# A conditioned two-layer decoder on one core: features a step earlier, shorter norms, and other first loads

## Chip, core and metric

The kernel runs on one core of one Trainium2 chip. The metric is the device time of one execution in microseconds (us); the time given for a kernel is the median of its runs.

## What is computed

Two transformer layers of width 2048 over 256 tokens, float32, batch 1. Every layer is a mixer and a squared-ReLU MLP of hidden width 8192, each with a modulated norm ahead of it and a gate behind it:

```
for l in (0, 1):
    shift, scale, gate, shift2, scale2, gate2 = split(silu(c) @ ada_w[l] + ada_b[l])   # 12288 columns
    h = rms_norm(x, norm_mix_g[l]) * (1 + scale) + shift
    x = x + gate * mixer(l, h)          # 0: MoBA + sliding window (GQA, sinks); 1: FoX + NSA
    h = rms_norm(x, norm_mlp_g[l]) * (1 + scale2) + shift2
    x = x + gate2 * (relu(h @ up[l]) ** 2 @ down[l])
out = rms_norm(x, final_norm_g)
```

The even mixer projects h to 4608 columns: eight MoBA heads' q, k and v, and eight sliding-window q heads with two k and v heads; with 256 tokens MoBA is causal attention inside one block.

## The kernel before

**Data.** x is kept transposed in xT: 16 feature blocks of 128, each 128 x 256 tokens. The modulated, normed features are in xs, per block a float32r high part (256 columns) and the rest, the low part (256 columns). A matrix product is three matmuls per pair of blocks: high x high, low x high, high x low.

**Weights.** `load` (L312) brings weights in pieces of 128 x 1024 words (0.5 MB) into the pool wst, tag "w", of eight buffers. ACT copies each piece to its high part wh (L319), DVE subtracts for the low part wl (L321). The wl instruction frees the buffer. All weight loads are issued by SP, in order.

**Modulation (ada).** `queue` puts one generator per section pair or column range into the list fill; `ada` (L222) is the generator. Sections are 0 shift, 1 scale, 2 gate of the mixer, 3, 4, 5 the same of the MLP. Each step loads 0.5 MB of ada_w into a wst buffer and multiplies it with cond: on PE (row, L238) where tensor is True, else on DVE (acc, L242 and L245, 128 x 1024). After the last step `columns` (L256) puts blocks into the list late: four transposes on PE, a reduction (L265) and a few small DVE instructions that write mod. `tick` (L293) is called once per weight load: it takes one entry of late and pumps 2 x rate steps of ada. `need(left, keys)` (L301) pumps until the sections named are through, and empties late.

**First layer's projection.** `even` (L615) goes over five groups of feature blocks, K1_GROUPS = 2, 2, 4, 4, 4 blocks, named 0 to 4 here. A group has nine calls of `kproj` (L374), each of which loads 512 columns of W for the group's blocks, ticks, seeds its PSUM tiles with the sum so far, multiplies and copies the sum out. The features of group g need the shift and scale of its columns; groups 0 and 1 have them from PE steps, 2 to 4 from DVE steps:

```
for g, (k0, kn) in enumerate(K1_GROUPS):
    need(end - g, (0, 1))
    ia, iv = make_h(0, 0, 1, Rs, range(k0, k0 + kn))
    rate[0] = R_K1[g]
```

In group 4 the sixteen attention heads follow their projections (`swa`, `moba`). `up_streamed` (L671) does the same for the first half of the first MLP's up projection: four groups of four blocks, eight kprojs each.

**Norms.** `residual` adds to xT and squares it on ACT (L147); DVE adds the squares to sacc (L151). `sumsq` (L440) sums over partitions by matmuls with ones (L444, L445), per half j of the tokens first sacc, then the last square t. `rstd` (L433) takes the power on POOL (L437). `norm_scale` (L448) makes the diagonal dg on DVE (L453) and multiplies ones with it (L454), so that R holds each token's factor on all partitions; with keep, ACT copies R to Rs (L456). `make_h` (L459) makes per block t = xT * scale * R on DVE (L463), high on ACT (L464), low on DVE (L465). `lazy_h` (L470) leaves it to `proj` (L348) to make four blocks per group of weights. `down` (L499) is the output and down projection: four blocks of columns, four weight loads and ticks each.

**Order.** Each engine runs its instructions in the order chosen when the kernel is built, by the program's order and by when an instruction could start by then-known costs; `issue_after` adds an order between two instructions of one engine.

**Start.** SP issues constants, x in eight loads of 128 x 512 (L162) into the pool big, and the tables of C_TRI (L163); ACT issues c and the small rows (L164 to L168). After group 0's make_h ACT issues the tables cos, sin and masks (L205) and the sinks. `norm_scale` here needs ones, which are in C_TRI.

Of the kernel before, what the change touches and what calls it, by code (L numbers as in the profile page):

```python
# [12 lines left out]
F32 = mybir.dt.float32  # L13
# [27 lines left out]
R_K1 = (0.6, 0.75, 0.9, 0.9, 1.6)  # L41
# [41 lines left out]
def build(tc, consts, x, c, norm_mix_g, norm_mlp_g, ada_w, ada_b, mlp_up, mlp_down, even_w_in, even_sinks,  # L83
# [5 lines left out]
    with ctx:  # L89
# [68 lines left out]
        xtok = [[None] * 4 for _ in range(2)]  # L158
        for q in range(4):
# [19 lines left out]
        for q in range(4):  # L179
            for j in range(2):  # L180
                junk = wrk.tile([128, 1024], F32, tag="acc", name="junk")
                A.activation(junk[:, 0:512], xtok[j][q], AF.Square, accum_out=ssq[:, 4 * j + q:4 * j + q + 1])
            for h in range(2):
                ps = psm.tile([128, 2, S], F32, tag="mm", name="xps")
                k0 = 4 * q + 2 * h
                for kk in range(2):
                    for j in range(2):
                        T.transpose(ps[:, kk, 128 * j:128 * j + 128], xtok[j][q][:, 128 * (2 * h + kk):128 * (2 * h + kk) + 128], ident)
                V.tensor_copy(xT[:, k0:k0 + 2, :], ps)
        ss0 = s32()  # L190
        V.tensor_reduce(ss0[:, 0:2], ssq[:, 0:8].rearrange("p (j q) -> p j q", q=4), AX.X, ALU.add)
# [12 lines left out]
        def later_vectors():  # L204
            A.dma_start(cst[:, 0:C_TRI], consts[:, 0:C_TRI])  # L205
            srow = att.tile([1, 8], F32, tag="srow", name="srow")
            A.dma_start(srow, even_sinks)
            A.dma_start(fb, fox_forget_b.rearrange("o h -> h o"))
# [13 lines left out]
        def ada(l, secs, c0, cw, tensor):  # L222
            cols = cw * len(secs)
            kn = KS * 512 // cols
# [4 lines left out]
            for t in range(KT // kn):  # L229
                w = wst.tile([128, kn, cols], F32, tag="w", name="wa")  # L230
                for z, s in enumerate(secs):
                    SP.dma_start(w[:, :, cw * z:cw * z + cw], ada_w[l, 128 * kn * t:128 * kn * (t + 1), D * s + c0:D * s + c0 + cw].rearrange("(k p) n -> p k n", p=128))
                for i in range(kn):
                    k = kn * t + i
                    hold = after("V")
                    if tensor:
                        q = 32 * (k % 4)
# [710 lines left out]
```

## Time and profile before

| | |
|---|---|
| median of 3 runs | 2288.84 us (2287.96 to 2292.45) |
| profiled execution | 2290.15 us |
| its span, first to last instruction | 2288.4 us |
| mean granted clock of TensorE | 0.985 of full |
| busy: PE, PEld, DVE, ACT | 97%, 94%, 73%, 52% |
| DMA | 600.06 MB, mean 262 GB/s |

PE is TensorE's matmuls, PEld its weight loads, DVE VectorE, ACT ScalarE, POOL GpSimd, SP SyncE, which only issues. L399 is line 399 of the kernel. PEclk is the granted TensorE clock as a share of 2.4 GHz; it is granted at that or at 1.2 GHz. An entry "[4.54 <-ACT xs L464]" means that the engine stood idle for 4.54 us and that the instruction of line 464 on ACT, which writes xs, ended it. PE's busy time runs together where matmuls overlap, so the count behind x is the better measure of its work.

### The profile page before, as it was taken

The numbers are of one execution on the slowest core, as the hardware profiler recorded it, in microseconds if no ns is written. First come the engines' busy times: TensorE is split into PE (matmuls) and PEld (weight loads), VectorE is DVE, ScalarE is ACT, GpSimd is POOL, SyncE is SP. The second block draws the span as 40 slices with busy tenths as digits, with TensorE's granted clock in tenths as the row PEclk, the third lists the DMA queues.
The fourth block names the chain that finished last, engine by engine and source line by source line (L and its number), as shares of the span: only waits on it lengthen the run. The fifth ranks groups of instructions, "written<-read, shape, count | busy, mean of one in ns | idle before, by whom it ended". The sixth has DMA issues, their size and how long they took to land.

```text
span 2288.4 us, 45838 instructions
## 1 busy us (share of the span) xinstructions
PE 2216.7 (97%) x18602; PEld 2147.1 (94%) x18602; DVE 1662.1 (73%) x2341; ACT 1180.4 (52%) x1873; POOL 5.6 (0%) x25
## 2 busy tenths in 40 slices
PE   8899999899999999999999999999999999999998
PEld 4799889899999999999999989899999999999997
DVE  3887899988877788887777977887545555555555
ACT  3766974578844354354454555444444444443543
POOL 0000000000000000000000000000000000000000
PEclk9999999999999999999999999999999999999999
DMA  9999679999998988988858876985555656555652
GB/s 320 312 333 322 242 258 364 326 355 364 328 317 276 319 290 300 312 306 295 262 184 296 313 253 222 325 313 159 193 198 190 199 190 201 188 198 189 199 185 93
DMA packets 296246, 600.06 MB, mean 262 GB/s; under 512 B 24706, under 2 KB 41954, under 8 KB 296034
## 3 DMA queue, kind: packets, MB, share of 16 engines
q1 hardware_dynamic: 295488, 596.38, 76.5%
q8 instruction: 146, 2.39, 0.4%
q10 hardware_dynamic: 546, 0.75, 0.1%
q14 instruction: 66, 0.54, 0.1%
HBM read 594.95 MB, written 2.10 MB: 261 GB/s over the span
## 4 chain that ended last, share of the span: by engine, by line
PE 47%; issue 33%; DVE 8%; DMA 7%; ACT 4%; SPq 0%; DVEq 0%; POOLq 0%; POOL 0%; ACTq 0%
PE mm L333 30%; PE mm L399 12%; DMA wa<-in_ada_w_dram 5%; DVE wl L321 3%; DVE acc L245 2%; PE bank L399 1%; ACT wh L319 1%; DMA w<-in_odd_w_in_dram 1%; PE row L238 1%; DMA w<-in_even_w_in_dram 1%; PE cps L263 1%; ACT u L402 1%; ACT mm L383 0%; PE bank L605 0%; ACT hs L417 0%
## 5 line engine op out<-in xcount | busy, mean ns | idle before, releaser
L321 DVE TENSOR_TENSOR wl<-w,wh 128x1024 fp32r<-128x1024 f32 x736 | 881.6, 1221 | 421.3 <-ACT wh L319 417.2
L319 ACT ACTIVATE wh<-w 128x1024 fp32r<-128x1024 f32 x736 | 754.1, 1055 | 771.4 <-PE mm L333 666.6
L333 PE MATMUL mm<-hs,wh 128*128 128x256 f32 x5120 | 881.3, 277 | 0.4 <-DVE xT L481 0.4
L333 PEld LDWEIGHTS mm<-hs,wh 128*128 128x128 f32 x5120 | 772.6, 188 | 1.6 <-DVE xT L481 1.0
L333 PE MATMUL mm<-xs,wh 128*128 128x256 f32 (+1 forms) x4128 | 717.8, 279 | 3.1 <-ACT xs L464 3.0
L333 PE MATMUL mm<-hs,wl 128*128 128x256 f32 x2560 | 708.3, 277 | 4.1 <-DVE wl L321 4.1
L333 PEld LDWEIGHTS mm<-xs,wh 128*128 128x128 f32 (+1 forms) x4128 | 626.3, 188 | 6.4 <-ACT xs L464 4.5
L333 PE MATMUL mm<-xs,wl 128*128 128x256 f32 x2064 | 571.7, 278 | 0.4 <-DVE wl L321 0.3
L245 DVE SCALAR_TENSOR_TENSOR acc<-wa,cond,acc 128x1024 f32<-128x1024 f32 x330 | 423.1, 1282 | 98.1 <-DMA wa<-in_ada_w_dram 96.3
L333 PEld LDWEIGHTS mm<-hs,wl 128*128 128x128 f32 x2560 | 481.0, 188 | 5.1 <-DVE wl L321 4.9
L333 PEld LDWEIGHTS mm<-xs,wl 128*128 128x128 f32 x2064 | 387.6, 188 | 1.5 <-DVE wl L321 1.0
L399 PE MATMUL mm<-xs,wh 128*128 128x256 f32 x1792 | 315.2, 280 | 6.0 <-ACT wh L319 4.2
L399 PEld LDWEIGHTS mm<-xs,wh 128*128 128x128 f32 x1792 | 273.2, 190 | 16.4 <-ACT wh L319 5.4
L399 PE MATMUL mm<-xs,wl 128*128 128x256 f32 x896 | 249.1, 279 | 1.5 <-DVE wl L321 1.5
L399 PEld LDWEIGHTS mm<-xs,wl 128*128 128x128 f32 x896 | 169.2, 190 | 2.2 <-DVE wl L321 2.1
L402 ACT ACTIVATE u<-mm 128x512 f32<-128x512 f32 x144 | 84.1, 592 | 73.9 <-PE mm L399 73.0
L383 ACT ACTIVATE mm<-u 128x512 f32<-128x512 f32 x112 | 65.5, 597 | 1.2
L548 ACT ACTIVATE t<-mm 128x256 f32<-128x256 f32 x96 | 36.5, 380 | 31.5 <-PE mm L333 26.2
L147 ACT ACTIVATE t<-xT 128x256 f32<-128x256 f32 x60 | 24.6, 415 | 51.3 <-DVE xT L481 51.3
L577 ACT ACTIVATE p<-p,st 128x128 f32<-128x128 f32 (+1 forms) x96 | 40.1, 420 | 19.7 <-DVE st L591 10.0
L399 PE MATMUL mm<-wh,xs 128*128 128x256 f32 x256 | 49.4, 286 | 0.1
L343 PE MATMUL mm<-wh,xs 128*128 128x256 f32 (+1 forms) x128 | 43.7, 342 | 0.0
(213 smaller groups left out, 1408.4 us busy)
## 6 DMA issues: line engine op xcount, KB each, us to landing
wa<-in_ada_w_dram SPq DMA_DIRECT2D x256, 512.0 KB, 5.2
w<-in_mlp_up_dram SPq DMA_DIRECT2D x256, 512.0 KB, 4.4
w<-in_mlp_down_dram SPq DMA_DIRECT2D x256, 512.0 KB, 4.9
wa<-in_ada_w_dram SPq DMA_DIRECT2D x256, 256.0 KB, 5.1
w<-in_odd_w_in_dram SPq DMA_DIRECT2D x88, 512.0 KB, 4.7
w<-in_even_w_in_dram SPq DMA_DIRECT2D x72, 512.0 KB, 5.4
w<-in_even_w_out_dram SPq DMA_DIRECT2D x32, 512.0 KB, 5.7
w<-in_odd_w_out_dram SPq DMA_DIRECT2D x32, 512.0 KB, 5.5
```

The costliest lines, as they stand in the source:

```text
L147: A.activation(s, xT[:, kt, :], AF.Square)
L238: T.matmul(row[q:q + 32, :], cond[:, k:k + 1].to_broadcast([128, 32]), w[:, i, :], start=k < 4, stop=k >= KT - 4, tile_position=(0, q))
L245: V.scalar_tensor_tensor(acc, w[:, i, :], cond[:, k:k + 1], acc, op0=ALU.mult, op1=ALU.add)
L319: A.activation(wh, w, AF.Copy)
L321: V.tensor_tensor(wl, w, wh.bitcast(F32), op=ALU.subtract)
L333: T.matmul(P[0:m, 0:S], st[:, c0:c0 + m], mv, start=f and i == 0, stop=e and i == 2)
L343: T.matmul(Ps[j][:, 0:n], lo, wh[:, c0:c0 + n], start=False, stop=e)
L383: A.activation(P, flat[i], AF.Copy)
L399: T.matmul(Ps[i][:, 256 * h:256 * h + 256], st, mv, start=first and e == 0, stop=last and e == 2, skip_group_check=True)
L402: A.activation(flat[i], P, AF.Copy)
L548: A.activation(r, P[:, 0:S], AF.Relu)
L577: A.activation(p[:, o:o + n], p[:, o:o + n], AF.Exp, bias=m[:, i:i + 1], accum_out=den[:, i:i + 1])
```

## The change

The features of the next group are made ahead of the group's last kproj (groups of four blocks) or last two (groups of two) in `even`, and ahead of the last kproj in `up_streamed`; the rates of groups 0 and 1 rise. ada loads shift and scale in one load where a step has one feature block, and in groups 0 and 1, whose steps are now twice as large, each section into its own buffer; the order of the two sections is turned. The norm's factor comes from a matmul of the broadcast r with the identity, without dg; R is always copied to Rs; `sumsq` takes sacc for both halves first; the last load of the last column block of a `down` that ends in a norm has no tick. The first `proj` behind a `lazy_h` goes over the feature blocks outermost for its first group. x comes in four loads of 128 x 1024 into wst; C_TRI comes with the later tables, which SP issues at the end of group 1.

```
-R_K1 = (0.6, 0.75, 0.9, 0.9, 1.6)
+R_K1 = (0.65, 0.9, 0.9, 0.9, 1.6)
...
-                xtok[j][q] = big.tile([128, 512], F32, tag="b", name="xtok")
-                SP.dma_start(xtok[j][q], x[0, 128 * j:128 * j + 128, 512 * q:512 * q + 512])
-        SP.dma_start(cst[:, C_TRI:C_ID], consts[:, C_TRI:C_ID])
...
+        xtok = [[wst.tile([128, 1024], F32, tag="w", name="xtok") for _ in range(2)] for _ in range(2)]
+        for q in range(2):
+            for j in range(2):
+                SP.dma_start(xtok[q][j], x[0, 128 * j:128 * j + 128, 1024 * q:1024 * q + 1024])
...
         def later_vectors():
-            A.dma_start(cst[:, 0:C_TRI], consts[:, 0:C_TRI])
+            SP.dma_start(cst[:, 0:C_ID], consts[:, 0:C_ID])
...
         def ada(l, secs, c0, cw, tensor):
             cols = cw * len(secs)
-            kn = KS * 512 // cols
+            split = len(secs) == 2 and cw == 256
+            kn = KS * 512 // (cw if split else cols)
...
+                for z, s in enumerate(secs if split else secs[0:1]):
+                    w = wst.tile([128, kn, cw if split else cols], F32, tag="w", name="wa")
+                    if kn == 1:
+                        SP.dma_start(w[:, 0, :].rearrange("p (s n) -> p s n", n=cw), src[:, 0, secs[0]:secs[-1] + 1, c0:c0 + cw])
                     else:
+                        SP.dma_start(w, src[:, :, s, c0:c0 + cw])
...
+            fresh = len(hgen) == 4
...
+                if fresh and g == 0:
+                    for k in range(4):
+                        for mt in range(4):
+                            mm_T(Ps[0][1][mt], ws[k:k + 1], 128 * mt, 128, xs_rhs(k, 1), k == 0, False)
+                    continue
...
-            for j in range(2):
-                T.matmul(ps[:, j:j + 1], sacc[:, 128 * j:128 * j + 128], ones[:, 0:1], start=True, stop=False)
-                T.matmul(ps[:, j:j + 1], sq[:, 128 * j:128 * j + 128], ones[:, 0:1], start=False, stop=True)
+            for t in (sacc, sq):
+                for j in range(2):
+                    T.matmul(ps[:, j:j + 1], t[:, 128 * j:128 * j + 128], ones[:, 0:1], start=t is sacc and j == 0, stop=t is sq and j == 1,
+                             skip_group_check=True)
...
-            dg = t256()
             for j in range(2):
-                V.tensor_scalar(dg[:, 128 * j:128 * j + 128], ident, r[:, j:j + 1], None, op0=ALU.mult)
-            T.matmul(R[:, 0:S], ones, dg, start=True, stop=True)
-            if keep:
-                A.activation(Rs, R[:, 0:S], AF.Copy)
+                T.matmul(R[:, 128 * j:128 * j + 128], r[:, j:j + 1].to_broadcast([128, 128]), ident, start=True, stop=True)
+            A.activation(Rs, R[:, 0:S], AF.Copy)
...
+                with tc.issue_after(done[-2]) if len(done) > 1 else nullcontext():
+                    V.scalar_tensor_tensor(t, xT[:, k, :], mod[:, 6 * l + sc, k:k + 1], R, op0=ALU.mult, op1=ALU.mult)
...
-                hgen.append(lambda g=g: make_h(l, sh, sc, R, range(4 * g, 4 * g + 4)))
+                hgen.append(lambda g=g: make_h(l, sh, sc, Rs if g else R, range(4 * g, 4 * g + 4)))
...
-                    tick()
+                    if not (sums and blk == 3 and n == 3):
+                        tick()
...
+            def features(g):
+                need(end - g, (0, 0))
+                k0, kn = K1_GROUPS[g]
+                return make_h(0, 0, 1, Rs, range(k0, k0 + kn))
+
+            features(0)
             for g, (k0, kn) in enumerate(K1_GROUPS):
-                need(end - g, (0, 1))
-                ia, iv = make_h(0, 0, 1, Rs, range(k0, k0 + kn))
...
                     kproj(W, g, 512 * b, [(256 * i, "T", qa[b][i]) for i in range(2)], k0, kn)
+                    if b == 1 and g < end and kn == 2:
+                        features(g + 1)
                     kproj(W, g, 1024 + 512 * b, [(256 * i, "T", ka[b][i]) for i in range(2)], k0, kn)
...
+                    if b == 1 and g < end and kn == 4:
+                        features(g + 1)
                     kproj(W, g, 2048 + 512 * b, [(0, j, va[b][j]) for j in range(2)], k0, kn)
...
-                if g == 0:
-                    with tc.issue_after(ia.ins):
-                        srow = later_vectors()
+                if g == 1:
+                    srow = later_vectors()
+                if g == 2:
                     sinks(srow)
...
                 for b in range(4 * K2C):
+                    if g < 3 and b == 4 * K2C - 1:
+                        features(g + 1)
```

## Rows read from the trace of the kernel before

**Rows 1.** The page's first part: busy time, share of the span and instructions of each engine.
```profile
PE 2216.7 (97%) x18602; PEld 2147.1 (94%) x18602; DVE 1662.1 (73%) x2341; ACT 1180.4 (52%) x1873; POOL 5.6 (0%) x25
```

**Rows 2.** Table by stretch (A:B length, engines' busy us, PEclk, DMA share, GB/s).
```profile
core 0: us, PE busy (x) PEld busy (x) DVE busy (x) ACT busy (x) POOL busy (x), PEclk, DMA share, GB/s
28.00:222.00 194.00, 175.85 (x1377) 162.55 (x1378) 143.12 (x158) 126.89 (x189) 0.00 (x0) 0.95 0.91 323
107.00:164.00 57.00, 53.19 (x441) 52.96 (x442) 48.15 (x52) 39.39 (x59) 0.00 (x0) 0.95 0.95 340
164.00:222.00 58.00, 56.16 (x459) 53.80 (x459) 44.73 (x47) 37.46 (x55) 0.00 (x0) 0.95 0.85 299
180.00:200.00 20.00, 20.00 (x177) 20.00 (x176) 17.20 (x15) 14.93 (x22) 0.00 (x0) 1.00 1.04 383
222.00:260.00 38.00, 37.93 (x285) 30.15 (x285) 25.23 (x62) 28.97 (x65) 0.00 (x0) 1.00 0.80 278
260.00:318.00 58.00, 50.61 (x359) 45.81 (x358) 53.17 (x126) 51.93 (x120) 0.00 (x0) 0.97 0.64 222
318.00:412.00 94.00, 93.98 (x808) 92.64 (x806) 92.24 (x127) 43.73 (x69) 0.00 (x0) 1.00 0.99 353
484.00:534.00 50.00, 50.00 (x443) 50.00 (x442) 45.26 (x48) 39.66 (x59) 0.00 (x0) 1.00 0.99 356
```

**Rows 3.** PE's waits, whole span (who <- what ended it: us, times, longest).
```profile
PE bank L399 <- ACT xs L464: 10.8, 4, 4.5
PE aux L454 <- DVE t L453: 7.1, 4, 2.6
...
PE aux L444 <- DVE sacc L151: 4.2, 3, 3.1
PE mm L333 <- ACT xs L464: 3.0, 3, 1.1
```

**Rows 4.** Timeline at the boundary from group 1 to 2 (start us, us, engine, line).
```profile
106.14 1.27 DVE L463 SCALAR_TENSOR_TENSOR t<-xT,mod,sacc 128x256 f32<-128x256 f32 x3
...
107.22 0.58 PE L399 MATMUL bank<-xs,wh 128*128 128x256 f32 x1 [4.54 <-ACT xs L464]
```

**Rows 5.** Table by stretch, around that boundary and around the first norm.
```profile
104.00:112.00 8.00, 4.78 (x23) 4.79 (x24) 8.00 (x17) 4.28 (x8) 0.00 (x0) 0.57 0.71 217
415.00:426.00 11.00, 7.80 (x34) 6.74 (x35) 9.32 (x17) 2.20 (x5) 1.62 (x1) 0.53 0.77 275
```

**Rows 6.** The chain that ended last: a stretch of group 2, one of group 4.
```profile
115.18 44.03 PE mm L399 x384
...
245.22 1.84 PE row L238 x12
```

**Rows 7.** What SP's queue waited for before issuing, 0 to 222 us.
```profile
SPq L232 <- DVE wl L321: 32.7, 23, 3.7
...
SPq L232 <- DMA cst<-in_consts_dram: 5.6, 1, 5.6
SPq L232 <- DMA xtok<-in_x_dram: 3.9, 2, 2.8
```

**Rows 8.** The page's costliest groups: busy us, mean ns of one behind the bar.
```profile
L321 DVE TENSOR_TENSOR wl<-w,wh 128x1024 fp32r<-128x1024 f32 x736 | 881.6, 1221 | 421.3 <-ACT wh L319 417.2
...
L245 DVE SCALAR_TENSOR_TENSOR acc<-wa,cond,acc 128x1024 f32<-128x1024 f32 x330 | 423.1, 1282 | 98.1 <-DMA wa<-in_ada_w_dram 96.3
```

**Rows 9.** Timeline of SP's queue at the start.
```profile
9.16 11.01 SPq L232 DMA_DIRECT2D wa<-in_ada_w_dram  x16
```

**Rows 10.** Timeline at the first norm (behind the even layer's output projection).
```profile
415.59 0.57 PE L444 MATMUL aux<-cst,sacc 128*128 128x1 f32 x2
...
418.51 0.48 DVE L453 TENSOR_SCALAR t<-cst,s 128x128 f32<-128x128 f32 x2 [0.58 <-POOL s L437]
...
420.37 0.38 ACT L456 ACTIVATE sacc<-aux 128x256 f32<-128x256 f32 x1 [5.51 <-PE aux L454]
420.79 1.26 DVE L463 SCALAR_TENSOR_TENSOR t<-xT,mod,aux 128x256 f32<-128x256 f32 x3 [0.60 <-ACT sacc L456]
```

**Rows 11.** Timeline at the second norm (ahead of the odd layer's mixer).
```profile
1142.65 1.26 DVE L463 SCALAR_TENSOR_TENSOR t<-xT,mod,aux 128x256 f32<-128x256 f32 x3 [0.85 <-PE aux L454]
```

More of the change, by code (lines that the diff above doesn't have):

```diff
@@ L229, in ada @@
             for t in range(KT // kn):
[L230 to L237, printed above, removed]
-                        T.matmul(row[q:q + 32, :], cond[:, k:k + 1].to_broadcast([128, 32]), w[:, i, :], start=k < 4, stop=k >= KT - 4,
-                                 tile_position=(0, q))
-                    elif k == 0:
-                        with hold:
-                            V.tensor_scalar(acc, w[:, i, :], cond[:, 0:1], None, op0=ALU.mult)
-                    else:
-                        with hold:
-                            V.scalar_tensor_tensor(acc, w[:, i, :], cond[:, k:k + 1], acc, op0=ALU.mult, op1=ALU.add)
+                src = ada_w[l, 128 * kn * t:128 * kn * (t + 1), :].rearrange("(k p) (s n) -> p k s n", p=128, n=D)
@@ new lines, in ada @@
+                for z, s in enumerate(secs if split else secs[0:1]):
+                    w = wst.tile([128, kn, cw if split else cols], F32, tag="w", name="wa")
+                    if kn == 1:
+                        SP.dma_start(w[:, 0, :].rearrange("p (s n) -> p s n", n=cw), src[:, 0, secs[0]:secs[-1] + 1, c0:c0 + cw])
+                    else:
+                        SP.dma_start(w, src[:, :, s, c0:c0 + cw])
+                    for i in range(kn):
+                        k = kn * t + i
+                        hold = after("V")
+                        if tensor:
+                            q, n = 32 * (k % 4), cw if split else cols
+                            T.matmul(row[q:q + 32, n * z:n * z + n], cond[:, k:k + 1].to_broadcast([128, 32]), w[:, i, :],
+                                     start=k < 4 and z == 0, stop=k >= KT - 4 and (not split or z == 1), tile_position=(0, q), skip_group_check=True)
+                        elif k == 0:
+                            with hold:
+                                V.tensor_scalar(acc, w[:, i, :], cond[:, 0:1], None, op0=ALU.mult)
+                        else:
+                            with hold:
+                                V.scalar_tensor_tensor(acc, w[:, i, :], cond[:, k:k + 1], acc, op0=ALU.mult, op1=ALU.add)
@@ L672, in up_streamed, with features @@
             us = [u_tile() for _ in range(8 * K2C)]
+            def features(g):
+                need(3 - g, (l, 3))
+                return make_h(l, 3, 4, Rs if g else R, range(4 * g, 4 * g + 4))
+            ia, iv = features(0)
             for g in range(4):
-                need(3 - g, (l, 4))
-                ia, iv = make_h(l, 3, 4, Rs if g else R, range(4 * g, 4 * g + 4))
                 for b in range(4 * K2C):
+                    if g < 3 and b == 4 * K2C - 1:
+                        features(g + 1)
                     if g == 0 and b == 2 and GATE:
@@ L894, in build @@
         for g in range(4):
-            queue(0, (4, 3), False, 512 * g, 512)
+            queue(0, (3, 4), False, 512 * g, 512)
         for c0 in (0, 1024):
```

36 lines of the change are left out of this document (17 added, 19 removed).

## The prediction

> **What bounds the kernel now.** I read the page's engine shares first: PE is busy 97% of the span, so a change can win only where PE stands still or runs at a low clock [rows 1]. The table by stretch comes next: in the first layer's projection groups (28 to 222 us) PE has 175.9 of 194 us busy at 0.95 of its clock, while the DMA engines are 91% busy; in group 4 with its attention it has 37.9 of 38 and then 50.6 of 58; in the output projection after it (318 to 412) it has it all [rows 2]. What ends PE's waits in these groups is the feature step: four waits for the first xs, 10.8 us; the norms' waits on dg and on sacc add 7.1 and 4.2 us [rows 3]. The boundary at 107 us shows why: DVE starts the features at 106.14, only then, and PE starts at 107.22 after 4.54 us of nothing [rows 4]; the clock around it is 0.57 of full, so matmuls on both sides of the wait ran at the lower level of 1.2 GHz for part of the time [rows 5]. Without a wait, 384 matmuls take 44.03 us, 0.1147 each [rows 6].
>
> **Features a kproj or two earlier.** A group of four feature blocks is nine kprojs of 48 matmuls: 432 x 0.1147 = 49.5 us. The group that begins at 107 lasts 57 us and the next one 58 [rows 2, 4]; so about 16 us are over in these two, boundary waits, low clock and transposes together. With features(g+1) ahead of the last kproj, their cover is that kproj, 5.5 us of matmuls, against 8 x 0.42 = 3.4 us of DVE work for four blocks (three of their eight instructions take 1.27 us [rows 4]). What they need must be there: the ada steps of the next group. Before, nine ticks a group at the old rates pump 10.8 + 13.5 + 16.2 + 16.2 = 56.7 steps, and groups 1 to 4 need 8 + 16 + 16 + 16 = 56, so the last step comes at the boundary itself. After, the rates give 11.7 + 16.2 + 16.2 + 16.2 = 60.3, and 4 + 48 = 52 are needed (group 1's steps are twice as large), with the last one two or three ticks before features. The wait at the boundary should go; late next is the DMA.
>
> **What that costs the DMA.** (60.3 + 4) - 56.7 = 7.6 steps of 0.524 MB, 4.0 MB, are loaded ahead of group 4 that were not; the table adds 0.2 MB here (a step is 128 x 1024 words of 4 bytes). From 28 to 222 us the queues moved 323 GB/s x 194 us = 62.7 MB; now 66.9 MB. The tiles' release paces it: SP waits longest for DVE's wl [rows 7]. If the tiles in waiting at the end of group 3 are 2 MB fewer (they pile up at a boundary), 64.9 MB are to be moved. Rates seen: 323 over the groups, 340 in group 2, 353 in the output projection, which asks for as much, 383 in the best 20 us [rows 2]. I take 350, nearest to the stretch without boundaries: 185 us. DVE allows it: in group 2 it is busy 48.2 of 57 us, of which 18 wl at 1.22 and 16 acc at 1.28 are 42 [rows 2, 8], so some 51 us a group is its floor.
>
> **The first loads.** The first ada load goes out at 9.16 us, and its group's sixteen take 11.01 us to issue [rows 9]; SP waits 3.9 us for x landings and later 5.6 us for the tables, which go out on the other queue [rows 7]. Four x loads for eight, eight ada loads for sixteen, and the tables later on SP's own queue take most of it away. xtok now takes four of the eight w slots, so half of group 0's ada waits for the transposes: bounded by 0 and 6 us of gain, I take 4, by the 3.9 us row. One load in place of two at the other ada steps saves SP's issue time alone, which hides beside the waits above: 0.
>
> So group 4 begins at 28 - 4 + 185 = 209 to 211 us instead of 222: **-11 us**.
>
> **The last group.** About eight steps of section 2 on PE are already done, and eight more steps on DVE come in here. PE: three steps took 1.84 us on the chain [rows 6], so eight are 4.9 us off the front, where PE is bound (37.9 of 38 us). DVE: 8 x 1.28 = 10.3 us; it has 12.8 us idle in the first 38 us, but is busy 53.2 of 58 in the rest [rows 2]. Bounds: -5 (all covered, PE's part gained) and +10.3 (nothing covered). About half of the new steps fall in the first part: +5, less 3 of PE's 4.9: **+2 us**.
>
> **Norms.** In the first, without the last tick two accs of 1.28 us no longer stand among the sacc adds, against a wait of 3.1 us: 1.5 (0 to 2.5; wl of the next stage may take their place). Without dg, whose two instructions take 0.48: 0.5. Both sacc products ahead of both of t: 0.4 of the second pair's 0.57 [rows 10]. Of 11 us at 0.53 of the clock [rows 5] a shorter standstill may spare 1.0 (0 to 1.7). Sum **-3.4** (-0.9 to -5.1). In the second and third the same 0.5 and 0.4 go, but now R is copied there too: in the first norm it was ACT's copy, 0.38 us, that released DVE's first feature, in the second, without copy, PE itself [rows 10, 11]. So +0.4 each: **-0.5** each, **-1.0**. The Trainium skill (PSUM — Partial Sum Buffer, "PSUM bank collisions raise a hardware error") says that reads of one bank by two engines must be kept apart as well; by that the copy and the feature cannot be side by side, and the 0.4 stays; were they free to overlap, it would be -1.8 in place of -1.0. Blocks outermost in the first proj (fresh): 0, bounds 0 and -1.5: only three waits there in all, 3.0 us, are for xs [rows 3], and some of them stand at the very first block. Features ahead of the last kproj in up_streamed, the order inside make_h: 0, bounds -0.5 and +3 (three boundaries at one wl of 1.22), as PE is busy there in all of 50 us [rows 2]. Rest of the program: 0, give or take 2, from shifted ada steps.
>
> **Sum.** -11 + 2 - 3.4 - 1.0 = -13.4 us. The profiled execution took 2290.15 us, which gives 2276.7; it is 1.3 us over the median of the three runs, 2288.84. On that median: **2275 us**.
>
> **Rivals.** *The DMA gains little* (18%): 340 GB/s as in group 2 and no fewer tiles in waiting: 66.9 / 0.340 = 197 us, group 4 starts 1 us earlier, and -1 + 2 - 4.4 = -3.4: 2285. For it: DMA is 91% busy already. Against it: 353 and 383 elsewhere. *The extra load decides* (8%, slower): the rate stays at the groups' own 323, because slots, not boundaries, hold it: 66.9 / 0.323 = 207 us, group 4 starts at 231, +9 + 2 - 4.4 = +6.6: 2295. It ends slower once the rate is under about 334 (66.9 MB in 200 us). Against it: at the boundaries the queue is seen to drop, 299 in group 3 against 383 inside it [rows 2]. *The DMA runs as in its best stretch* (16%): 66.9 MB at 383 GB/s, 175 us; PE's own floor, 3 x 49.5 and some 15 us for the steps on PE, is not in the way: group 4 at 199, -23, and with 0 for the last group -27.4: 2261. The Trainium skill (DMA: Bandwidth & Descriptors, Specifications) gives about 358 GB/s as the memory's limit for a core; by it 66.9 MB take 187 us, group 4 starts at 211, and this rival is out. The trace does not agree: 383 over 20 us. *The change doesn't move the work* (4%): engines' orders are fixed when the kernel is built, and the features may end up where they were; then loads and norms gain 4 + 4.4, against 2 in the last group and 4.2 MB at 350 GB/s, 12 us, half of it in the boundaries' gaps: 2288.
>
> **How the numbers follow.** The forecast has 54%; its own range is 2265 to 2284 (rates of 343 to 360 give -9 to -18 for group 4's start; the bounds of the last group halved, norms). A measurement of this kernel can tell about 0.2%, 4.6 us, from no change. Faster by more: 54 + 16 + 10 of the first rival's 18 (its time lies on the border) = 80%. Within: 8 + 4 = 12%. Slower: 8%. The range 2263 to 2287 leaves out the slower rival, a good third of the 383 rival and the forecast's tails.
>
> **What would show it.** Right: no wait of PE's for xs over 2 us between groups; stretch rows of the groups over 340 GB/s; first matmul of the groups 4 us earlier, group 4 near 210, the output projection's end some 9 us earlier; PE's standstill at the first norm halved; DVE waiting for ACT's copy in all norms. Wrong: PE waits for wl or wh inside groups 0 and 1 that add up to the old boundary waits (DMA), acc of L245 before 260 us absent and the attention longer (last group), or new waits in up_streamed.

## The result and the profile after

The changed kernel takes **2301.86 us** (median of five runs, 2300.14 to 2306.16) against 2288.84 for the kernel before (2286.04 to 2294.68): ratio 1.0052, 95% interval 1.0034 to 1.0069. It is 13 us slower; the forecast was 2275, with 8% for slower. The profiled execution took 2306.16 us with a span of 2304.4, 16.0 more than the span of before; it is the slowest of the five, 4.3 us over their median, where that of before is 1.3 us over its own.

Where the 16.0 us come from is read from the timeline, as the start of the first matmul of each stage (us from the span's start; "best" is the kernel i2 below):

| first matmul of | before | after | best |
|---|---|---|---|
| group 0 | 29.6 | 26.1 | 25.7 |
| group 2 | 107.2 | 112.6 | 104.9 |
| group 4 | 221.8 | 229.4 | 221.9 |
| first norm | 415.1 | 431.3 | 408.9 |
| the up-projection behind it | 421.9 | 437.0 | 414.8 |
| second norm | 1138.7 | 1155.7 | 1133.7 |
| third norm | 1565.8 | 1581.1 | 1560.7 |
| end of the span | 2288.4 | 2304.4 | 2284.0 |

The start is 3.5 us earlier; the forecast had 4. Groups 0 to 3 then take 203.3 us instead of 192.2, and group 4 with the output projection 201.9 instead of 193.3. All of the loss in the profiled executions lies ahead of the first norm; behind it the kernels keep step within 2 us.

Table by stretch of the changed kernel, its groups 0 to 4 and the output projection (columns as in [rows 2]):

```profile
core 0: us, PE busy (x) PEld busy (x) DVE busy (x) ACT busy (x) POOL busy (x), PEclk, DMA share, GB/s
26.10:66.10 40.00, 35.09 (x280) 29.22 (x277) 21.28 (x27) 19.63 (x30) 0.00 (x0) 0.93 0.98 340
66.10:112.60 46.50, 34.35 (x226) 31.24 (x224) 34.45 (x39) 29.96 (x50) 0.00 (x0) 0.89 0.92 324
112.60:169.10 56.50, 55.19 (x442) 54.08 (x443) 47.05 (x50) 34.62 (x51) 0.00 (x0) 0.94 0.89 307
169.10:229.40 60.30, 60.30 (x490) 52.66 (x488) 37.33 (x42) 39.78 (x60) 0.00 (x0) 1.00 0.95 327
229.40:326.00 96.60, 84.34 (x601) 76.25 (x600) 80.29 (x178) 78.13 (x175) 0.00 (x0) 0.95 0.70 234
326.00:431.00 105.00, 98.81 (x827) 97.49 (x825) 100.75 (x147) 49.00 (x79) 0.00 (x0) 0.97 0.95 339
...
26.10:229.40 203.30, 184.92 (x1433) 167.21 (x1430) 140.10 (x156) 123.99 (x188) 0.00 (x0) 0.95 0.93 323
```

The same view of the kernel before, its groups 0 and 1, and 0 to 3:

```profile
29.60:66.60 37.00, 36.95 (x254) 28.10 (x255) 16.03 (x23) 20.00 (x30) 0.00 (x0) 0.95 0.92 325
66.60:107.20 40.60, 29.54 (x226) 27.69 (x224) 32.95 (x34) 29.65 (x48) 0.00 (x0) 0.93 0.94 331
...
29.60:221.80 192.20, 175.65 (x1377) 162.35 (x1377) 141.47 (x151) 126.10 (x187) 0.00 (x0) 0.95 0.91 323
```

Compare the last line of each first: 323 GB/s in 192.2 us before, 323 GB/s in 203.3 us after. The queues did not get faster by a single GB/s; 62.1 MB became 65.7 MB, and 3.6 MB at 323 GB/s are 11.1 us, as much as the groups lost. That is a sum that fits and not yet a cause: e1, f2, f4 and i2 below move 65.7 or 65.8 MB in groups 0 to 3 too, in 193 to 196 us.

What sets the changed kernel apart lies in groups 0 and 1. They take 86.5 us for 77.6, groups 2 and 3 take 116.8 for 114.6. By the order of SP's queue, 31 loads of ada (counted in pieces of 0.5 MB) are issued within groups 0 and 1, against 24 before and 28 in those four kernels, which take 76.5 to 79.2 us for the two groups. DVE does 45 steps of the form acc<-wa,cond,acc in groups 0 to 3 of the kernel before, of e1 and of the changed kernel alike, but 15, 18 and 21 of them fall in groups 0 and 1.

The boundary waits, for whose sake the step was made, are gone. Waits of the changed kernel in its first 230 us (who waits, what ended it: us, times, longest):

```profile
PE mm L408 <- ACT wh L322: 8.1, 7, 2.1
PE mm L408 <- DVE wl L324: 6.4, 11, 1.2
...
PE bank L408 <- ACT wh L322: 2.4, 1, 2.4
...
PE bank L408 <- DVE wl L324: 1.3, 2, 0.6
```

and of the kernel before in its groups, beside the wait for xs of [rows 3]:

```profile
PE mm L399 <- ACT wh L319: 4.2, 2, 2.1
PE mm L399 <- DVE wl L321: 2.2, 4, 0.8
```

No wait for xs is left of the 10.8 us of [rows 3], but PE now waits 18.2 us for weights in place of 6.4. So PE's waits have hardly grown, 18.2 for 17.2 us: they have moved into groups 0 and 1, where PE is idle 16.8 us for 11.0, at a granted clock of 0.91 for 0.94. The rest of the 11.1 us stands in PE's busy time, and the rows don't divide it further; part of it is the gate's row matmuls, some of which are now done ahead of group 4.

"Waits for weights" does not mean waits for the DMA. What ACT waited for in groups 0 to 3 (29 to 222 us before, 0 to 230 us in the changed kernel), the kernel before first:

```profile
ACT u L402 <- PE mm L399: 44.3, 28, 5.8
...
ACT wh L319 <- DMA w<-in_even_w_in_dram: 0.9, 1, 0.9
```
```profile
ACT u L411 <- PE mm L408: 63.7, 27, 7.6
...
ACT wh L322 <- DMA w<-in_even_w_in_dram: 1.4, 2, 1.1
```

ACT stands idle for loads of weights for 1.4 us in all, and 63.7 us in front of evictions, for PE's last matmuls. Of the 42 weight loads of groups 0 to 3 whose landing the trace of the changed kernel has, 37 lay landed for 2 us or longer before ACT took them.

How a boundary looks now, timeline of the changed kernel at the end of group 1 (start us, us, engine, line; in brackets the idle time ahead and what ended it):

```profile
102.98 0.60 ACT L411 ACTIVATE u<-mm 128x512 f32<-128x512 f32 x1 [2.75 <-PE mm L408]
...
104.58 0.50 PE L408 MATMUL mm<-wh,xs 128*128 128x256 f32 x2 [0.86 <-ACT wh L322]
...
109.21 0.60 ACT L411 ACTIVATE u<-mm 128x512 f32<-128x512 f32 x1 [3.19 <-PE mm L408]
...
111.53 3.88 ACT L322 ACTIVATE wh<-w 128x1024 fp32r<-128x1024 f32 x4
112.60 2.36 DVE L324 TENSOR_TENSOR wl<-w,wh 128x1024 fp32r<-128x1024 f32 x2 [5.62 <-ACT wh L322]
112.62 0.50 PE L408 MATMUL bank<-xs,wh 128*128 128x256 f32 x2 [2.39 <-ACT wh L322]
```

Read it from the bottom. PE starts group 2 after 2.39 us of nothing because wh came late. wh came late because ACT stood in the eviction of the kproj before (L411), waiting 3.19 us for PE's last matmuls; the four wh run in a row, without a gap, and the trace has their loads landed at 101.9 to 108.3 us. DVE was idle for 5.62 us behind the same wh. While no tile is read none comes free. The table by stretch shows the queue and PE's clock there:

```profile
98.00:104.00 6.00, 4.86 (x24) 4.46 (x24) 4.81 (x7) 3.25 (x7) 0.00 (x0) 0.72 1.03 390
104.00:112.00 8.00, 4.89 (x24) 4.48 (x24) 2.42 (x2) 4.75 (x9) 0.00 (x0) 0.79 0.76 263
110.00:115.00 5.00, 1.97 (x10) 1.56 (x10) 2.40 (x3) 4.97 (x7) 0.00 (x0) 0.82 0.17 54
```

54 GB/s for five microseconds. So at this boundary a PE that waits for weights, part of the time at 1.2 GHz (granted clock 0.79), delays the eviction, the eviction delays wh, wh delays wl and the release of tiles, and only then does the queue fall. The Trainium skill (PSUM — Partial Sum Buffer, "Engine vs sequencer instructions") says that the queues of ScalarE and VectorE are strictly first in, first out; the trace agrees with it here: wh stands behind an eviction that it has nothing to do with.

In group 4 it is DVE. Its scale-and-shift steps, groups by line of the kernel before from 221.8 to 309.9 us:

```profile
L245 DVE SCALAR_TENSOR_TENSOR acc<-wa,cond,acc 128x1024 f32<-128x1024 f32 x10 | 12.8, 1281 | 0.0
...
L242 DVE TENSOR_SCALAR acc<-wa,cond 128x1024 f32<-128x1024 f32 x1 | 0.8, 755 | 0.0
...
L238 PE MATMUL row<-wa,cond 128*32 128x512 f32 x46 | 8.0, 602 | 0.0
```

and of the changed kernel from 229.4 to 326:

```profile
L248 DVE SCALAR_TENSOR_TENSOR acc<-wa,cond,acc 128x1024 f32<-128x1024 f32 x17 | 21.7, 1279 | 0.0
L245 DVE TENSOR_SCALAR acc<-wa,cond 128x1024 f32<-128x1024 f32 x2 | 1.5, 742 | 0.0
...
L241 PE MATMUL row<-wa,cond 128*32 128x512 f32 x22 | 3.8, 603 | 0.0
```

Eight steps more on DVE (19 for 11), as counted in the forecast, and 24 row matmuls fewer on PE, six steps for the eight or so of the forecast; but the stretch from group 4 to the first norm grew by 8.6 us, not by 2. PE's longest waits in the same two windows, before and after:

```profile
PE bank L581 <- DVE p L598: 1.3, 1, 1.3
```
```profile
PE mm L408 <- DVE wl L324: 8.5, 3, 4.2
```

Before, PE's list has no wait for wl in group 4; now it has 8.5 us, and the granted clock is 0.95 [table above]: DVE comes late with the weights' low parts.

The norms, first PE's waits over the whole span, then the first norm's timeline and its table by stretch:

```profile
PE aux L454 <- DVE sacc L151: 2.7, 3, 1.6
```
```profile
434.24 1.22 PE L462 MATMUL aux<-cst,s 128*128 128x128 f32 x4 [1.95 <-POOL s L446]
435.50 0.38 ACT L463 ACTIVATE sacc<-aux 128x256 f32<-128x256 f32 x1 [3.92 <-PE aux L462]
435.92 0.87 DVE L472 SCALAR_TENSOR_TENSOR t<-xT,mod,aux 128x256 f32<-128x256 f32 x2 [2.28 <-ACT sacc L463]
```
```profile
431.30:442.30 11.00, 7.30 (x39) 6.63 (x40) 8.64 (x15) 2.89 (x7) 1.55 (x1) 0.69 0.63 200
```

The longest wait for sacc is 1.6 instead of 3.1 us [rows 3], the clock around the norm 0.69 instead of 0.53 [rows 5], and DVE waits for ACT's copy before the first feature, as forecast. From the first sum to the first matmul behind it the three norms take 5.7, 5.2 and 4.7 us instead of 6.7, 5.1 and 5.4.

### The profile page after: what moved, and what is told of

Its sections match the earlier page's. It is cut to its first block, busy times and chain, and to the rows that moved or that the text cites. A ratio compares the mean times of both kernels' runs of the same rounds, so it can differ in the third digit from the quotient of the medians.

```text
span 2304.4 us, 45760 instructions
## 1 busy us (share of the span) xinstructions
PE 2221.4 (96%) x18674; PEld 2158.1 (94%) x18674; DVE 1659.5 (72%) x2333; ACT 1180.4 (51%) x1867; POOL 5.3 (0%) x25
## 3 DMA queue, kind: packets, MB, share of 16 engines
q8 instruction: 146, 2.39, 0.4%
## 4 chain that ended last, share of the span: by engine, by line
PE 49%; issue 33%; DVE 9%; DMA 6%; ACT 3%; POOL 0%; SPq 0%; DVEq 0%; POOLq 0%; ACTq 0%
PE mm L336 29%; PE mm L408 13%; DMA wa<-in_ada_w_dram 4%; DVE wl L324 3%; DVE acc L248 2%; PE bank L408 1%; ACT wh L322 1%; PE cps L266 1%; PE row L241 1%; DMA w<-in_odd_w_in_dram 1%; ACT p L588 0%; PE mm L346 0%; PE mm L345 0%; PE bank L616 0%; PE mm L344 0%
## 5 line engine op out<-in xcount | busy, mean ns | idle before, releaser
L248 DVE SCALAR_TENSOR_TENSOR acc<-wa,cond,acc 128x1024 f32<-128x1024 f32 x330 | 422.6, 1281 | 98.1 <-DMA wa<-in_ada_w_dram 96.2
L411 ACT ACTIVATE u<-mm 128x512 f32<-128x512 f32 x144 | 84.7, 593 | 94.4 <-PE mm L408 93.3
L392 ACT ACTIVATE mm<-u 128x512 f32<-128x512 f32 x112 | 64.9, 599 | 1.1
L268 DVE TENSOR_REDUCE s<-cps 128x4 f32<-128x512 f32 (+1 forms) x48 | 30.8, 643 | 21.8 <-PE cps L266 21.8
```

The costliest lines, as they stand in the source:

```text
L248: V.scalar_tensor_tensor(acc, w[:, i, :], cond[:, k:k + 1], acc, op0=ALU.mult, op1=ALU.add)
L268: V.tensor_reduce(red[:, 4 * b:4 * b + 4], src, AX.X, ALU.add)
L392: A.activation(P, flat[i], AF.Copy)
L411: A.activation(flat[i], P, AF.Copy)
```

## The experiments

Each kernel was run beside the kernel before on the same chip, and ratios are to that; the rounds (e, f, h, i) ran on different chips, so across rounds the ratios are compared and not the times. The runs of one kernel lie 5 to 18 us apart, so one profiled execution settles differences of some microseconds only where its waits show them too. For e1, f2, f4, h2, h3 and h4 it is the fastest of their runs. And since each engine's order is chosen anew for every kernel that is built, an edit can move work far from where it stands; no run separates that from its intended effect.

**Rates.** e1 is the changed kernel with the old rates:

```
-R_K1 = (0.65, 0.9, 0.9, 0.9, 1.6)
+R_K1 = (0.6, 0.75, 0.9, 0.9, 1.6)
```

> The changed kernel with the old rates of groups 0 to 3 (0.6, 0.75, 0.9, 0.9) and nothing else undone. Theory A (the raised rates put 4 MB and some eight DVE steps ahead of or into group 4, and the DMA rate does not rise): 3.6 steps, 1.9 MB, fewer come before group 4, at 0.33 MB a us some 5 to 6 us, and three or four DVE steps of 1.28 leave group 4's DVE: 8 to 10 us less than the changed kernel, near 2293. Rival B (the features placed ahead of the last kproj hold up wl and wh): no more than 2 us of difference. Rival C (the larger split ada steps of groups 0 and 1 fill the buffers): some 2 to 4 us, all in groups 0 and 1.

Measured: 2294.92, ratio 1.0013 (1.0001 to 1.0025). Group 4 begins at 221.5 instead of 229.4, with 1.9 MB less asked for ahead of it (three loads fewer in groups 0 and 1); the bytes moved by then are the same, since loads run ahead. In groups 0 and 1 PE is idle 12.7 us for 16.8, at a clock of 0.93 for 0.91, and they take 78.6 us for 86.5: the whole difference.

f1 is the opposite: the kernel before with the changed rates alone (the same line, turned round).

> The kernel before with the changed rates alone. Theory 'every load ahead of group 4 is paid for' (the groups are paced by their loads, not by the boundary waits): 3.6 steps of 0.524 MB more are asked for through group 3, 1.9 MB at 323 GB/s = 5.9 us, so group 4 begins at 226 to 229 us in place of 221.8, and the time is 2294 to 2298 (ratio 1.002 to 1.004). Rival 'only the new shape of the step makes it dear' (early features or one-section loads): the boundary waits give the queue time, group 4 begins before 224 and the ratio is within 0.001 of 1.

Measured: 2295.46, ratio 1.0024 (1.0013 to 1.0036); group 4 begins at 228.3. The rates by themselves cost 6.5 us (f1 against before) to 7.9 us (the changed kernel against e1) ahead of group 4. PE's waits from 26 to 228 us in f1, and from 26 to 222 us in f2 (below):

```profile
PE mm L399 <- ACT wh L319: 5.4, 3, 2.1
PE mm L399 <- DVE wl L321: 4.6, 10, 0.8
...
PE bank L399 <- DVE wl L321: 2.1, 4, 0.8
PE bank L399 <- ACT xs L464: 1.8, 1, 1.8
```
```profile
PE mm L408 <- ACT wh L322: 6.4, 6, 2.1
PE bank L408 <- ACT wh L322: 3.1, 1, 3.1
PE mm L408 <- DVE wl L324: 2.5, 6, 0.5
...
PE bank L408 <- DVE wl L324: 1.3, 2, 0.6
```

In f1 the features are still made at the boundary, and yet their wait has fallen from 10.8 to 1.8 us; in f2 it is gone. It was not the place of the call: PE waited for the last scale-and-shift step. Both edits that bring this step earlier, the rates in f1 and the form of the loads in f2 (against 9.5 us in e4 below), take the wait away, and it comes back as waits for wh and wl.

**The early features.** e3 is the changed kernel with the features of groups 1 to 4 made at the boundary again:

```
-            features(0)
             for g, (k0, kn) in enumerate(K1_GROUPS):
+                features(g)
...
-                    if b == 1 and g < end and kn == 2:
-                        features(g + 1)
...
-                    if b == 1 and g < end and kn == 4:
-                        features(g + 1)
```

> The changed kernel with the first layer's features made at the group's boundary again, rates and loads as changed. Theory A: the waits for the features come back at the boundaries, slower than the changed kernel by 0 to 10 us, since the DMA then catches up in them. Rival B (the early features cost more than they save): faster than the changed kernel by 3 us or more.

Measured: 2297.88, ratio 1.0028 (1.0018 to 1.0039), 0.24% under the changed kernel's ratio, though the intervals overlap by a little. The same edit alone lies between e1 and f2 (1.0013 and 1.0035; f2 is introduced next) and between f4 and i2 below (0.9978 and 0.9960). It is not always on the same side, and in none of the six profiles does PE wait more than 0.2 us for xs in the groups: the early call in `even` does nothing that these runs can tell.

**The form of the loads.** e4 has the groups of the kernel before (its rates, its features at the boundary and its body of `ada`), and of the change only the first loads, the norms, `up_streamed` and the order of sections. f2 is e4 with the changed body of `ada`. From the changed kernel to f2, besides the edit of e3:

```
-R_K1 = (0.65, 0.9, 0.9, 0.9, 1.6)
+R_K1 = (0.6, 0.75, 0.9, 0.9, 1.6)
```

and from f2 to e4:

```
-            split = len(secs) == 2 and cw == 256
-            kn = KS * 512 // (cw if split else cols)
+            kn = KS * 512 // cols
...
+                w = wst.tile([128, kn, cols], F32, tag="w", name="wa")
+                for z, s in enumerate(secs):
+                    SP.dma_start(w[:, :, cw * z:cw * z + cw], ada_w[l, 128 * kn * t:128 * kn * (t + 1), D * s + c0:D * s + c0 + cw].rearrange("(k p) n -> p k n", p=128))
```

> The first layer's groups as before (ada's loads and steps, rates, features at the boundary), with the new first loads, norms, down without last tick, and up_streamed's early features kept. All theories that put the loss into the groups: first matmul 3.6 us earlier than before, groups as long as before, norms 1 to 2 us better, the whole 3 to 6 us under the kernel before, near 2284. Rival D (first loads or the table's new place cost as well): at or above the kernel before.

> As e4, but with the changed form of the scale-and-shift loads (both sections in one load, or a section at a time where a group has two blocks). Theory 'every load is paid for': the bytes are those of e4, so the ratio is that of e4, 1.000 plus or minus 0.0015, group 4 begins at 222 plus or minus 2. Rival 'the form costs': a tile of one section is held until both have come, group 0 and 1 get longer by 2 us or more each and the ratio is 1.002 or more. Rival 'half the issues help': group 4 begins before 219.

Measured: e4 2291.99, ratio 1.0002 (0.9991 to 1.0013): loads and norms, 8.4 us in the forecast, bring nothing that shows in the time, as my rival D has it. Its first matmul is 2.7 us earlier than before, and group 4 begins at 222.1; from there to the first norm it takes 198.2 us for 193.3, with 46 steps on DVE for 47, and why stays open. f2: 2299.91, ratio 1.0035 (1.0022 to 1.0048), though its profiled execution, its fastest, has group 4 at 222.2 and a span 2.1 us under that of e4. Of the three theories none fits both numbers, and h3 speaks the other way; what the form costs by itself stays open.

**Tiles or queue.** f3 is the changed kernel with a ninth tile for loads:

```
-NS = 8
+NS = 9
...
-            return tmp.tile([128, 2, S], F32, tag="t2", name="t2", bufs=2)
+            return tmp.tile([128, 2, S], F32, tag="t2", name="t2", bufs=1)
...
-            return att.tile([128, 32], F32, tag="st", name="st", bufs=4)
+            return att.tile([128, 32], F32, tag="st", name="st", bufs=3)
```

> The changed kernel with nine tiles for loads in place of eight (and one buffer fewer in two small pools of the attention). Theory 'tiles hold the queue back' (each tile waits for DVE's or PE's reading, so the rate is tiles over holding time): 9/8 of the tiles in flight raise the rate, and groups 0 to 3 go from 203 to 195 us or less. Rival 'the queue is at its limit for these loads': groups 0 to 3 stay at 203 plus or minus 1.5, and the tiles only wait longer.

Measured: groups 0 to 3 take 204.0 us, so a ninth tile does not help there. That is the rival's number, but not its reason: e1, f2, f4 and i2 move the same bytes at 335 to 340 GB/s, so the queue was not at its limit. Tiles are held because their readers are late. The time is 2355.80, ratio 1.0284 (1.0270 to 1.0298): the first MLP takes 761.6 us for 718.7. For that see the last section.

**Group 4.** e2 is the changed kernel with a lower rate in group 4:

```
-R_K1 = (0.65, 0.9, 0.9, 0.9, 1.6)
+R_K1 = (0.65, 0.9, 0.9, 0.9, 1.15)
```

> The changed kernel with group 4's rate at 1.15 in place of 1.6: eight steps fewer are pumped in group 4, all of them DVE steps. Theory A's second half (DVE steps beside the attention cost their whole duration): group 4 shorter by about 8 x 1.28 = 10 us, near its 88 us of the kernel before, and nothing changed ahead of it. Rival: group 4 is long since its weights come late, behind ada loads; then it also gets shorter, but by PE's waits on wl without DVE being less busy. Rival B: no change in group 4. The steps come back later, where DVE has room or not: the end may gain less than group 4 does.

Measured: from group 4 to the first norm 191.1 us instead of 201.9, with 44 steps on DVE for 53: 9 steps, 10.8 us, 1.2 each; a step takes 1.28. In the changed kernel nothing covered them, and PE's wait for wl in group 4 is gone; h2 below shows that this does not hold for the kernel before. But the odd layer takes 429.5 for 420.2, where they are made up for (90 steps for 82), and the ratio is 1.0025 (1.0011 to 1.0040).

f4 therefore gives them room in the first MLP, and has the old rates in groups 0 to 3:

```
-R_K1 = (0.65, 0.9, 0.9, 0.9, 1.6)
+R_K1 = (0.6, 0.75, 0.9, 0.9, 1.15)
...
-R_M0 = 0.6
+R_M0 = 0.66
```

> The changed kernel with the old rates in groups 0 to 3, 1.15 for 1.6 in group 4, and 0.66 for 0.6 in the first MLP, so that the eight DVE steps taken out of group 4 fall where PE has work for all of the time. Theory 'DVE steps cost their time in group 4 and nothing in the MLP': group 4 begins at 221.5 as in e1, the stretch from it to the first norm is 191 (as in e2), the MLP 717 plus or minus 2, the odd layer 421: 2282 to 2286, ratio 0.997 to 0.999. Rival 'a step costs its time wherever it is put': the MLP takes 10 us more or the odd layer 9 more as in e2, ratio 1.001 or more.

Measured: **2285.49, ratio 0.9978 (0.9969 to 0.9987)**. Group 4 begins at 219.2, the stretch to the first norm takes 184.9, the MLP 718.8, the odd layer 423.4. The time is as I expected, though the profiled execution, 3 us under the median, has the second stretch 6 us shorter than forecast. With the old rates in groups 0 and 1 and two numbers more, the changed kernel is faster than the kernel before.

**Is it the change or the two numbers?** h2 is the kernel before with the rates 1.15 and 0.66, h1 is f4 without the blocks outermost, h3 is f4 with the old body of `ada` (the second diff of e4), h4 is f4 with less still in group 4. The edits of h2, h1 and h4, in this order:

```
-R_K1 = (0.6, 0.75, 0.9, 0.9, 1.6)
+R_K1 = (0.6, 0.75, 0.9, 0.9, 1.15)
-R_M0 = 0.6
+R_M0 = 0.66
...
-            fresh = len(hgen) == 4
+            fresh = False
...
-R_K1 = (0.6, 0.75, 0.9, 0.9, 1.15)
+R_K1 = (0.6, 0.75, 0.9, 0.9, 0.9)
-R_M0 = 0.66
+R_M0 = 0.7
```

> The kernel before with nothing changed but the two rates of f4 (1.15 in group 4, 0.66 in the first MLP). Theory 'the change as a whole is worth nothing, and f4's gain is the spread of DVE steps': group 4 begins at 222, from it to the first norm 187 to 190 us in place of 193.3 (some 8 steps of 1.28 us less), ratio 0.997 to 0.999 as f4. Rival 'f4's gain is the changed kernel's, set free': ratio 1.000 plus or minus 0.001.

> f4 with the order of the kernel before in the first projection after a norm (tile of output outermost, the four blocks inside it). The last MLP took 717.2 us from its first matmul in the kernel before and 718.3 to 719.0 in every kernel with the blocks outermost, while its norm was 0.5 to 0.7 shorter. Theory 'the new order gives the norm's gain back': the last MLP goes back to 717 to 717.5 and the norm's standstill stays at 4.7 to 4.9, time 1 to 2 us under f4's, ratio 0.997. Rival 'what the first block waits for is the same, the time is only booked behind its first matmul': standstill 5.2 to 5.5 and MLP 717 to 717.5, sum as in f4.

> f4 with the old form of the scale-and-shift loads (each tile holding both sections, two loads into it). Theory 'the form costs' (from f2 against e4, 1.0035 and 1.0002): 4 to 8 us less than f4, ratio 0.994 to 0.996. Rival 'f2's number is only the spread of its five runs': as f4, within 2 us, or 1 to 3 us more, since group 1's steps are eight again and three of group 4's are forced at the features.

> f4 with 0.9 in group 4 in place of 1.15 and 0.70 for 0.66 in the first MLP: 18 x 0.25 = 4.5 steps fewer in group 4. Theory 'a step of 1.28 us costs its time in group 4 and nothing in the MLP': group 4 up to the first norm 185 in place of 184.9 less 3 to 5 us, so 180 to 182 us, ratio 0.996. Rival 'what is taken out of group 4 comes back in the output projection, which needs the gate by then': group 4 is 4 us shorter and the stretch behind it 4 us longer, ratio as f4's.

Measured: **h2 2304.90, ratio 1.0066 (1.0053 to 1.0078)**, against both theories. It is 3 us ahead at the first norm (412.1), but it was so when group 4 began (218.5 for 221.8), up to which its rates are those of before. From group 4 to the first norm it takes 193.6 us for 193.3, with 39 steps on DVE for 47: in the kernel before, where PE does not wait for wl in group 4, eight steps fewer bring nothing. Then the MLP takes 736.0 us for 716.8. PE's waits from the first norm's end to 700 us in h2, and to 690 us in f4:

```profile
PE mm L399 <- ACT xs L464: 9.7, 3, 4.2
PE mm L333 <- DVE wl L321: 4.2, 4, 3.3
```
```profile
PE mm L336 <- DVE hs L427: 2.2, 1, 2.2
PE mm L408 <- ACT xs L473: 1.5, 1, 1.5
```

My reading was that with fewer steps done by the first norm the rest is forced out at the boundaries of `up_streamed`, and that the changed kernel, which makes these features a kproj early, hides it; i1 tests that. h1: 2285.51, ratio 0.9973 (0.9961 to 0.9984), the last MLP 718.4 as with blocks outermost: the new order is worth nothing either way, and both of my guesses on it fall. h3: 2294.83, ratio 1.0017 (1.0004 to 1.0030): here the old loads are worse, which neither expectation has. Two waits for xs, 3.8 us, are back in the groups, but the profiled execution is 11 us under the median, so what the other runs lost isn't seen. h4: 2295.42, ratio 1.0021 (1.0010 to 1.0031): from group 4 to the first norm 183.5 us, 1.4 less than f4, and 10.2 more in the MLP (729.0). Neither expectation has that. Of the three pairs of rates tried in the changed kernel (1.6, 1.15 and 0.9 in group 4), the middle one is the best.

**What was open.** i1 is f4 with the features of `up_streamed` at the boundary, i2 is f4 with those of groups 1 to 4 at the boundary (the edit of e3), i3 is h1 with fewer steps at first. The edits of i1 and i3:

```
-            ia, iv = features(0)
             for g in range(4):
+                ia, iv = features(g)
...
-                    if g < 3 and b == 4 * K2C - 1:
-                        features(g + 1)
...
-R_K1 = (0.6, 0.75, 0.9, 0.9, 1.15)
+R_K1 = (0.55, 0.7, 0.9, 0.9, 1.2)
```

> f4 with the features of the up-projection after the first norm made at the boundary again, as in the kernel before. Theory 'with fewer steps done by the first norm the rest is forced out in one go at each boundary, and only features made a kproj early hide that' (h2: 9.7 us of PE waits for xs and 23.3 us lost in the first five sixteenths of this stretch more than in the kernel before): the stretch from the first norm to the second goes from 718.8 to 730 to 737, ratio 1.003 to 1.006. Rival 'h2's loss came from the groups' old loads and order': 719 plus or minus 3, ratio 0.998.

> f4 with the features of groups 1 to 4 made at the boundary again, all else as in f4. Theory 'early features pay only where the loads keep up, and at these rates they nearly do': four waits for xs of 2 to 3.5 us come back, group 4 begins 2 to 6 us later than the 219.2 of f4, ratio 0.999 to 1.001. Rival 'the loads pace the groups either way, so early features are worth nothing': group 4 begins at 219 plus or minus 2 and the ratio is 0.998. Third: 'they cost': group 4 before 216, ratio under 0.997.

> h1 with the rates 0.55 and 0.70 for 0.60 and 0.75 in the first two groups (1.8 steps fewer, 0.94 MB) and 1.20 for 1.15 in group 4. Theory 'the first two groups are paced by the steps asked for in them': they get 2.8 us shorter (0.94 MB at 340 GB/s), of which 1 to 2 us are lost again where the missing steps are forced at the next features; group 4 begins 1 to 3 us earlier than in h1, ratio 0.996 to 0.9975. Rival 'forced steps cost what the others save': group 4 at 220.9 plus or minus 1, ratio as h1's 0.9973 or up to 1.000.

Measured: i1 2291.95, ratio 0.9996 (0.9984 to 1.0008), the MLP 727.9 with 5.8 us of waits for xs. That is between the two expectations: 9 us more than f4 in this stretch, half of what h2 lost in it, and 0.18% or 4 us by the ratios, whose intervals overlap by a little. So the early features of `up_streamed`, priced at 0 in the forecast, are worth 4 to 9 us at these rates, and they explain half of h2's loss; the other half is open.

i2: **2283.16, ratio 0.9960 (0.9944 to 0.9975), the best kernel of the study**, though its interval overlaps those of f4 and h1; it is 0.4% faster than the kernel before and, by the two ratios (0.9960 / 1.0052), 0.9% faster than the changed one. Its groups, and group 4 with the output projection, by stretch:

```profile
25.70:221.90 196.20, 179.93 (x1422) 163.98 (x1422) 140.99 (x153) 125.71 (x188) 0.00 (x0) 0.96 0.95 335
221.90:408.90 187.00, 177.72 (x1427) 166.76 (x1425) 168.48 (x313) 125.58 (x254) 0.00 (x0) 1.00 0.81 280
```

In the groups it waits 0.2 us for xs, with the features at the boundary. And it moves the same 65.7 MB as the changed kernel (196.2 x 335) in 7.1 us less: not the bytes decide but where they are asked for. All of the 7.1 us lie in groups 0 and 1 (79.2 us for 86.5; groups 2 and 3: 117.0 for 116.8). There a kproj has two blocks and 24 matmuls, half as many as a later one, to run beside a step of the same 1.28 us.

i3: 2296.08, ratio 1.0017 (1.0005 to 1.0028). Group 4 begins at 218.4, 2.5 us before h1's, as the theory has it, but the output projection takes 116 us for 105, and the time is beyond both expectations. DVE has two steps more in the output projection (35 for 33) and as many as h1 from group 4 to the first norm (42), so the steps alone don't explain 11 us; that stays open.

## Why the prediction was wrong

**The groups: the step that failed.** "I take 350, nearest to the stretch without boundaries: 185 us." Measured were 323 GB/s, to the digit the rate of before, and 203.3 us. The step priced the groups as MB over GB/s, with the DMA as what paces them. The trace has it the other way round: loads have landed and lie waiting, ACT waits 1.4 us for them in all, a ninth tile brings nothing, and the same 65.7 MB take 193 to 203 us in different kernels. What I took for idle time of the queue, caused by the boundary waits, was its pace behind its readers, ACT and DVE, which stand in order behind PE. f1 and f2 show that the boundary was not what held it: with the waits for xs all but gone, groups 0 to 3 do not get shorter (199.3 and 196.1 us, before 192.2). That the tiles in waiting would be 2 MB fewer did not come either: 65.7 MB were moved, not 64.9. *The extra load decides*, which I gave 8%, came nearest in its numbers: it has group 4 at 231 (229.4) and the rate at 323, but its total of 2295 is 7 us short, and its reason, that slots hold the rate, is not what f3 shows. The argument against it, 299 in group 3 against 383 inside, was that of the forecast itself: a best stretch shows what the queue can do, not what it would do for longer if one wait were gone. The limit of about 358 GB/s that the Trainium skill gives (DMA: Bandwidth & Descriptors, Specifications) decided nothing. The Trainium skill also says (Perfetto Trace Analysis, "Roofline") that a core can pull more than this share when it alone is active; the trace agrees, with 383 GB/s over 20 us [rows 2].

**"The wait at the boundary should go; late next is the DMA."** The first half is right; the second isn't: late next were wh and wl, on ACT and DVE, with their loads landed. The sign of being wrong that the prediction names, waits for wl or wh in groups 0 and 1, came true, but not for the reason that it puts behind it, the DMA. And the sentence put no price on where the added steps go: seven of the eight loads more are issued in groups 0 and 1, six of DVE's steps move there, and the waits that they bring cost as much as those that went.

**The last group.** +2 was taken, with 10.3 as the upper bound; measured +8.6. DVE's steps were counted right; "about half of the new steps fall in the first part", where DVE has idle time, was the error. PE waits 8.5 us for wl there, and e2 shows that the last nine steps are covered by nothing. h2 shows that this is no fixed price of a step: in the kernel before, eight fewer bring nothing, which fits a cover that the eleven steps of before had not used up and the nineteen did.

**First loads.** -4 was forecast, -3.5 seen, and lost again by group 4 in e4, whose groups 0 to 3 take 195.2 us for 192.2 with the same loads; why is not shown.

**Norms.** Right in mechanism, too large in size: of -3.4 at the first about 2.5 are seen (1.5 of the wait for sacc, 1.0 of the rest), the second gains nothing, the third 0.7; behind them 1.4 us are lost again, in the last MLP above all (718.6 for 717.2), whose cause stays open.

**The range** (2263 to 2287) ended under the rival's 2295. Both large terms were off in the same direction: 7.6 in place of -11, and 8.6 in place of +2.

## What to carry to other kernels

A wait that sits at a boundary is not idle time for the sake of taking: ask what the engines' other work does while it lasts, and what the thing waited for was itself late on. Where work is pumped in by rates, price each step in the stage in which it lands, by that stage's cover, and look at the stages with half the cover first. The steps that cost 1.2 us each in the changed kernel's group 4 cost far less in the MLP (718.8 us in f4, 713.2 to 718.7 in e1, e2 and the changed kernel, with ten to twelve steps fewer), and eight fewer brought nothing behind the start of group 4 in the kernel before. Before a queue is called the limit, look whether what it brings is waited for. Two parts of one change can hold each other up: here the lower rates brought 0.2% with the early features in `up_streamed` (f4), nothing without them (i1), and a loss in the kernel before (h2).

## What the runs showed of the hardware

With a ninth tile for loads the first MLP took 43 us longer, and all that lies ahead of it 2 us. DVE's mean times for wl and acc stay the same (1218 and 1281 ns), but from 450 to 1150 us DVE waits 123.1 us for scale-and-shift loads instead of 70.3, and the queues move 275 GB/s from 800 to 900 us for 296. Where the tiles lie in memory moved too, so the runs don't tell which of the two it is.

The queues go from 390 GB/s (98 to 104 us of the changed kernel) to 54 (110 to 115) within some ten microseconds, while four loads of weights that had landed by 108.3 us wait for ACT until 111.53 and later: here a rate over a stretch says more of the readers than of the queue.
